# A hybrid encoder layer on one core: the value products of a pair of attention heads, issued block by block or as one chain

## The chip, the core and the metric

The kernel runs on one core of a Trainium2 chip. The metric is the device time of one execution in microseconds (us), lower is better. TensorE (PE) multiplies matrices, VectorE (DVE), ScalarE (ACT) and GpSimd (POOL) do the work on rows, and SyncE (SP) issues every DMA of this kernel from one queue, in the order of the program. Each engine runs its instructions in the order in which they stand.

## The reference, cut to what matters

One layer reads 16 meta tokens, a prompt of 512 tokens and a sample of 2048 tokens, all float32 with 1024 features. One input projection feeds two groups of heads, and one output projection adds their result to the input.

```
proj = rms_norm(h) @ w_in                      # 1024 x 4624
q_m, k_m, v_m, o_m, z_m, gates, q_a, k_a, v_a, z_a = split(proj)
# group A: mLSTM in both directions, 4 heads of 128
q_m, k_m = silu(conv5(q_m, k_m));  h_m = scan_forward + scan_backward
y_m = rms_norm(sigmoid(o_m) * h_m) * silu(z_m)
# group B: attention on a grid of 64 columns, 8 heads of 64, window 8 rows x 16 columns + meta keys
s = rms_norm(q_a) . rms_norm(k_a) / 8 + bias   # masked to the window
y_a = (softmax(s) @ v_a) * silu(z_a)
out = h + concat(y_m, y_a) @ w_out
```

## The kernel before, in words

The program is written as generators that are stepped in turn (`weave`); a scheduler then puts the recorded instructions of each engine into an order of its own, which is fixed before the kernel runs. What stands in the tables of order below is that fixed order.

*Projections* (`mmt`, `mmf`, L233) multiply blocks of tokens by groups of 256 columns of `w_in`, three matmuls for each product (high and low parts). There are 7600 of them. The first half of the tokens comes first, then the second half; the last to come are the columns of the prompt. *Attention* (L478 on) runs over five windows of 8 grid rows (the name of a window's kind stands in `WINS`), and in each over four pairs of heads: 20 pairs. Windows 1 and 2 run beside the projections of the first half, windows 3, 4 and 0 beside those of the second half; the small window 0 is the last. For each pair the kernel

- loads keys `kt`, values `vt`, queries `qt` and bias rows `R`, transposes the keys into `kps` (two halves, L502) and splits them on ACT and DVE into `Ks`, and does the same for the queries (`qps`, L512);
- for each of four blocks of query columns, b = 1, 2, 0, 3, and each of the two heads: scores `sps` on PE (L546), bias and minimum on DVE (L549), exponential on ACT (L550), reciprocal and scaling on DVE (L551, L552), three or four transposes into `pps` (L555), and a copy into a buffer `pt` on ACT (head 0, L558) or DVE (head 1, L560);
- after the two heads of a block, multiplies with the values: `py<-pt,vt` (L564), 3 or 4 chunks by 2 heads. The stationary operand has 64 columns, and each head writes its own 64 partitions of `py`, so one head takes one half of the array's columns and the other head the other half. All other matmuls of this kernel load 128 columns (the meta tokens' 48 and a few small ones apart);
- at the end multiplies `py` with the gate rows `zt` (L571) and stores them.

There are three `pt` buffers, one `vt`, and two banks of PSUM for the tag `c`, which `kps` and `py` take in turn.

*The mLSTM* has a backward part, `mlstm_back`: 15 steps over the chunks of the sample from the last to the first, then 3 for the prompt. A step loads `kT` and `v` (one buffer each, tags of the pool `bp`), transposes the keys (`kpm`, L671), scales them on ACT (`kw`, L674), multiplies (`ups`, L684), updates the state `CB` on DVE (L690) and stores it (`cbs`, L704). It begins when all the sample's keys and values are through, and each step needs the one before. The forward part (`hps`, L781 and L783) and the output projections (`ops`, L843) come last: chunk 0 of the sample needs the state that the last backward step of the sample stored (`CBl<-cbs`). The attention's pool of SBUF is given back when attention is through (`tstack.close()`); the output weights (`wor`, eight loads of 512 KB through one buffer) and the buffers of the forward part are laid into it.

Of the kernel before, what the change touches and what calls it, by code (L numbers as in the profile page):

```python
# [26 lines left out]
# window geometry of the attention: kinds of row groups (P, first, middle, last)  # L27
# kind: (key rows, first key row, first query row, grid rows, row offset in the bias table)
# [39 lines left out]
def bcast(ap, n):  # L68
    """A DRAM row read by n partitions."""
    return bass.AP(tensor=ap.tensor, offset=ap.offset, ap=[[0, n]] + [list(x) for x in ap.ap])  # L70


def view(ap, dims):
    """A tile's partitions with free dimensions of one's own."""
    return bass.AP(tensor=ap.tensor, offset=ap.offset, ap=[list(ap.ap[0])] + [list(x) for x in dims])


class Rot:
    """a pool whose tags turn over n tiles (or k times as many)"""
# [8 lines left out]
class Run:  # L88
# [4 lines left out]
    def setup(self):  # L93
        nc, a = self.nc, self.a
        self.const = cp = self.ctx.enter_context(self.tc.tile_pool(name="const", bufs=1))
        self.dram = dp = self.ctx.enter_context(self.tc.tile_pool(name="scr", bufs=1, space=bass.MemoryType.DRAM))
        PS = bass.MemoryType.PSUM
        ent = self.ctx.enter_context
        self.ps_mm = ent(self.tc.tile_pool(name="ps_mm", bufs=2, space=PS))
        self.ps_a = ent(self.tc.tile_pool(name="ps_a", bufs=2, space=PS))  # L100
        self.ps_b = ent(self.tc.tile_pool(name="ps_b", bufs=2, space=PS))
        self.ps_c = ent(self.tc.tile_pool(name="ps_c", bufs=2, space=PS))

        self.ident = cp.tile([128, 128], F32, name="ident")
        make_identity(nc, self.ident)
        self.bg_rep = cp.tile([128, 16], F32, name="bg_rep")
        self.cw = cp.tile([128, 8, 5], F32, name="cw")
        self.gq = cp.tile([128, 1], F32, name="gq")
        self.gk = cp.tile([128, 1], F32, name="gk")
        self.mg = cp.tile([128, 4], F32, name="mg")  # L110
        self.gcol = cp.tile([84, 2, 8], F32, name="gcol")
        self.one = cp.tile([1, 128], F32, name="one")
        nc.vector.memset(self.one, 1.0)
        # gates: type, chunk (P 0-3, S 4-19, meta 20), head
        self.gates = cp.tile([128, 4, 21, 4], F32, name="gates")
        for ty, val in ((0, NEG), (1, 1e4), (2, NEG), (3, 1e4)):
            nc.gpsimd.memset(self.gates[:, ty, 20, :], val)
        self.kv = set()
        self.tails = cp.tile([128, 8, 4], F32, name="tails")
        self.mraw = cp.tile([128, 8, 20], F32, name="mraw")  # L120
        nc.vector.memset(self.mraw, 0.0)

        d = lambda name, shape, dt=F32: dp.tile(shape, dt, name=name)
        self.x2 = d("x2", [10, 128, KT * 128])
        # token rows: P 0-511, S 512-2559, meta 2560-2575
        # attention: by blocks of grid columns (16 or 8), then grid rows (P 0-7, S 8-39)
        self.qs = d("qs", [4, 40 * 16, 512])
        self.ks = d("ks", [8, 40 * 8, 512])
        self.vs = d("vs", [8, 40 * 8, 512])
        self.kmeta = d("kmeta", [8, 8, 512])  # L130
        self.vmeta = d("vmeta", [8, 8, 512])
        self.zs = d("zs", [512, 2560])
        self.vms = d("vms", [2576, 512])
        self.ozs = d("ozs", [2560, 1024])
        self.kqs = {"P": d("kqsP", [1024, NM + LP]), "S": d("kqsS", [1024, NM + LS])}
        self.yas = d("yas", [512, 2560])
        self.rp = d("rp", [88, 94])
        self.Rd = d("Rd", [128, 169, 32])
        self.Mrow = d("Mrow", [2, 84 * 128])
        self.cbs = d("cbs", [20, 128, 4 * 129])  # L140
# [12 lines left out]
    def bias_table(self, pool):  # L153
        """for a query at (qr, qc) of its tile: a head's relative key rows (15 of 22) and columns"""
        nc, s = self.nc, self.rp
        t = pool.tile([128, D], F32, tag="x", name="rpt", bufs=3)
        nc.sync.dma_start(out=t[:88, :94], in_=self.a["rpbp"].rearrange("h (i a) j -> (h i) (a j)", a=2))
        nc.sync.dma_start(out=s, in_=t[:88, :94])
        for qr in range(8):
            src = bass.AP(tensor=s.tensor, offset=s.offset + (7 - qr) * 47 + 15, ap=[[47, 169], [-1, 16], [1, 32]])  # L160
            nc.sync.dma_start(out=self.Rd[qr * 16:(qr + 1) * 16, :, :].rearrange("q i j -> i q j"), in_=src)
            yield

# [16 lines left out]
    def xprep(self, pool, srcs, put):  # L180
        """srcs: DRAM rows of up to 128 tokens each; put(i, k0, psum) takes the transposes."""
# [25 lines left out]
    def split(self, hi, lo, ps):  # L207
        """hi: ps rounded to float32r; lo: what is left."""
        self.nc.scalar.copy(out=hi, in_=ps)
        self.nc.vector.tensor_tensor(out=lo, in0=ps, in1=hi.bitcast(F32), op=ALU.subtract)  # L210

# [15 lines left out]
    def mm3(self, ps, st, mv, n_k=KT):  # L227
        """ps = sum over k of st^T mv, both as (hi, lo)."""
# [7 lines left out]
    # token-major product: 128 tokens by n columns  # L236
# [6 lines left out]
    # token-major product of the meta tokens: hi on the first 16 partitions, lo on those from 32  # L243
# [13 lines left out]
    # feature-major product: 128 columns by a block's tokens  # L257
# [82 lines left out]
    def phase_a1(self, blocks, pool, first=None):  # L340
        """first: weights of the first two column groups, which are then taken block by block"""
# [13 lines left out]
    def phase_a1_z(self, blocks, pool, done):  # L355
        """done: gets the groups of columns that are through"""
# [18 lines left out]
    def conv(self, pool, raw, n, ct):  # L375
        """silu of the five taps: n outputs from n + 4 inputs."""
# [10 lines left out]
    def phase_a2(self, blocks, pool, free=None):  # L387
        """free: is told of each block that is no longer needed"""
# [86 lines left out]
    def attention(self, pool, wins, zdone):  # L475
        nc, a = self.nc, self.a
        for wi in wins:
# [6 lines left out]
            for pair in range(4):  # L484
                f0 = pair * 128
                kt = pool.tile([128, 8, 128], F32, tag="kt", name="kt", bufs=1)
                vt = pool.tile([128, 8, 128], F32, tag="vt", name="vt", bufs=1)
# [9 lines left out]
                # keys: head A as [hi; lo], head B as [lo; hi]  # L497
# [11 lines left out]
                # queries: hi and lo, each twice over the partitions  # L509
# [13 lines left out]
                py = self.ps_c.tile([128, 512], F32, tag="c", name="py")  # L523
                biases = {}
                for b in (1, 2, 0, 3):
# [5 lines left out]
                    pts = []  # L531
                    for hh in range(2):
# [23 lines left out]
                        pt = pool.tile([128, 512], F32, tag="pt", name="pt", bufs=3)  # L556
# [4 lines left out]
                        pts.append(pt)  # L561
                    for c in range(nch):
                        for hh in range(2):
                            nc.tensor.matmul(py[hh * 64:(hh + 1) * 64, b * 128:(b + 1) * 128], vt[:nk, cbs[c], hh * 64:(hh + 1) * 64], pts[hh][:nk, c * 128:(c + 1) * 128], start=c == 0, stop=c == nch - 1)  # L564
                    yield
# [10 lines left out]
    def gate_rows(self, pool):  # L576
# [9 lines left out]
        for d in range(2):  # L586
            big = pool.tile([128, 8, 128], F32, tag="vt", name=f"gbig{d}", bufs=1)
# [23 lines left out]
            # rows: b_L, A_L, m before, m after  # L611
# [54 lines left out]
    def wk(self, pool, kT, n, d, c):  # L666
        """token-major keys times the chunk's state weights."""
# [9 lines left out]
    def state(self, pool, kw, v, n, d, c, old, new):  # L677
        """new = decay * old + kw^T [v 1]"""
# [13 lines left out]
    def mlstm_back(self, pool, seq):  # L692
        """states that the backward direction has on entering each chunk."""
# [13 lines left out]
    def mlstm_first(self, pool, keep, seq):  # L707
        """the state that the meta tokens leave"""
# [7 lines left out]
    def mlstm(self, pools, rest, first, C, pre0, pre1, out_proj):  # L716
        """pools, rest: of the chunks in turn; first: gives a sequence's first state; C, pre0, pre1: for the first chunks"""
# [10 lines left out]
    def mlstm_pre(self, pool, seq, i):  # L728
        """what a chunk needs beside the states"""
# [119 lines left out]
def weave(main, *others, until=None):  # L849
    """Steps main to its end, or until that of one of the others: (generator, steps per step of main)."""  # L850
# [19 lines left out]
def hymba(ctx, tc, a):  # L870
# [12 lines left out]
    def block_t(where, tag, n, **kw):  # L883
        """by tiles of 128 tokens"""
# [74 lines left out]
    def reload():  # L959
        """the second part's x into the blocks of the first as they come free"""  # L960
# [110 lines left out]
```

## Time and profile before

| what | value |
|---|---|
| device time, three runs | 1788.88, 1791.68, 1792.33 us; median 1791.68 |
| span of the profiled execution, first to last instruction | 1788.1 us |
| PE busy | 1727.4 us, 97% of the span |
| DVE, ACT, POOL busy | 62%, 44%, 28% of the span |
| granted TensorE clock, mean | 0.992 of full speed |

The profile gives one execution, and its span is the time that it shows; it lies 3.6 us under the median of the runs, within their spread of 3.5 us at the lower end. "Busy" of PE is the union of the modelled durations of its matmuls, which overlap, so what a matmul costs is read from the distance between the starts of neighbouring matmuls and not from its duration. A line such as `py<-pt,vt x10` stands for ten records; a float32 product (`py`, `ups`, `hps`, `sm`) leaves two records for each matmul, a transpose or a product of the split parts leaves one.

### The profile page before, as it was taken

What the parts mean: (1) busy time and instruction counts of PE and PEld (TensorE: products, weight loads), DVE (VectorE), ACT (ScalarE), POOL (GpSimd) and SP (SyncE); (2) the same over time, 40 slices, a digit from 0 to 9 for tenths busy, and PEclk for the clock granted to TensorE, in tenths of its full rate; (3) what the DMA queues carried; (4) which work ended last, traced back from release to release, by engine and by line L of the source; (5) the groups of instructions that cost most, each with busy time, mean ns of one, the idle gap of its engine ahead of it and who ended that gap; (6) DMA issues with size and microseconds to landing.
All of it is one profiled execution on the core that took longest, in us unless ns stands there. A gap on an engine that the chain in (4) does not pass through costs nothing. (4 is left out here: it accounts for less than half of the span.)

```text
span 1788.1 us, 33369 instructions
## 1 busy us (share of the span) xinstructions
PE 1727.4 (97%) x12316; PEld 1554.0 (87%) x12316; DVE 1115.2 (62%) x2984; ACT 779.4 (44%) x1835; POOL 496.9 (28%) x503
## 2 busy tenths in 40 slices
PE   6999999999999999999999999999989899989999
PEld 6999998889889998999888888889878888878887
DVE  8896124654654369861249889876564578776772
ACT  5442232433444265422236666665554444443430
POOL 4012222223312253212124443432443222221210
PEclk9999999999999999999999999999999999999999
DMA  5367422324234363423334454444777765546531
GB/s 185 122 225 169 124 82 91 98 61 122 85 98 127 95 196 115 122 71 88 94 114 128 124 168 127 121 133 123 238 242 210 239 197 180 190 165 200 176 121 71
DMA packets 265986, 251.93 MB, mean 141 GB/s; under 512 B 38663, under 2 KB 228943, under 8 KB 265823
## 3 DMA queue, kind: packets, MB, share of 16 engines
q1 hardware_dynamic: 265822, 249.80, 46.2%
q8 instruction: 97, 1.59, 0.4%
q14 instruction: 67, 0.54, 0.1%
HBM read 176.34 MB, written 76.17 MB: 141 GB/s over the span
## 5 line engine op out<-in xcount | busy, mean ns | idle before, releaser
L233 PE MATMUL mmt<-wh,xah 128*128 128x256 f32 (+1 forms) x1536 | 437.9, 285 | 5.8 <-ACT sq L319 2.8
L233 PE MATMUL mmt<-wl,xah 128*128 128x256 f32 (+1 forms) x1536 | 438.0, 285 | 0.0
L233 PE MATMUL mmt<-wh,xal 128*128 128x256 f32 (+1 forms) x1536 | 436.5, 284 | 0.0
L224 POOL TENSOR_TENSOR wl<-wr,wh 128x512 fp32r<-128x512 f32 (+1 forms) x184 | 252.1, 1383 | 626.3 <-ACT wh L223 597.0
L233 PEld LDWEIGHTS mmt<-wh,xah 128*128 128x128 f32 x1536 | 289.9, 189 | 9.5 <-ACT sq L319 3.9
L233 PEld LDWEIGHTS mmt<-wh,xal 128*128 128x128 f32 x1536 | 291.0, 189 | 1.9 <-issue 1.0
L233 PEld LDWEIGHTS mmt<-wl,xah 128*128 128x128 f32 x1536 | 289.8, 189 | 2.3 <-issue 1.5
L537 POOL TENSOR_TENSOR bias<-R,amask 128x384 f32<-128x384 f32 (+5 forms) x120 | 111.8, 944 | 246.7 <-DVE mx L549 129.5
L223 ACT CAST wh<-wr 128x512 fp32r<-128x512 f32 (+1 forms) x184 | 109.8, 621 | 141.8 <-DMA wr<-in_w_in 121.1
L382 DVE SCALAR_TENSOR_TENSOR acc<-craw,cw,acc 128x256 f32<-128x256 f32 (+2 forms) x192 | 156.3, 814 | 24.1 <-ACT acc L380 19.7
L233 PE MATMUL mmf<-xah,wh 128*128 128x512 f32 x384 | 153.5, 400 | 1.4 <-DVE zt L368 1.2
L233 PE MATMUL mmf<-xal,wh 128*128 128x512 f32 x384 | 153.4, 399 | 0.0
L233 PE MATMUL mmf<-xah,wl 128*128 128x512 f32 x384 | 152.7, 398 | 0.0
L550 ACT ACTIVATE s<-s,mx 128x384 f32<-128x384 f32 (+5 forms) x160 | 96.1, 601 | 82.7 <-DVE mx L549 73.1
L233 PE MATMUL mmt<-wh,xbh 128*128 128x256 f32 (+1 forms) x384 | 113.0, 294 | 5.9 <-ACT sq L325 3.6
L233 PE MATMUL mmt<-wh,xbl 128*128 128x256 f32 (+1 forms) x384 | 112.9, 294 | 0.0
L564 PE MATMUL py<-pt,vt 128*64 128x128 f32 (+3 forms) x1120 | 110.3, 283 | 2.0 <-DVE pt L560 2.0
L233 PE MATMUL mmt<-wl,xbh 128*128 128x256 f32 (+1 forms) x384 | 111.8, 291 | 0.0
L549 DVE CUSTOM_DVE_ANT_0 s<-sps,bias 128x384 f32<-128x384 f32 (+5 forms) x160 | 84.5, 538 | 37.8 <-PE sps L546 34.4
L564 PEld LDWEIGHTS py<-pt,vt 128*64 128x64 f32 (+3 forms) x1120 | 72.9, 136 | 30.4 <-issue 12.7
L520 DVE SCALAR_TENSOR_TENSOR ql<-qps,gq,qh 64x512 fp32r<-64x512 f32 x80 | 59.9, 749 | 62.9 <-ACT qh L519 61.4
L552 DVE TENSOR_SCALAR s<-s,mx 128x384 f32<-128x384 f32 (+5 forms) x160 | 96.7, 606 | 3.1
(238 smaller groups left out, 3795.3 us busy)
## 6 DMA issues: line engine op xcount, KB each, us to landing
wr<-in_w_in SPq DMA_DIRECT2D x176, 256.0 KB
ozs<-vbuf SPq DMA_DIRECT2D x40, 256.0 KB
X<-Mrow SPq DMA_DIRECT2D x20, 512.0 KB
oz<-ozs SPq DMA_DIRECT2D x20, 512.0 KB
v<-vms SPq DMA_DIRECT2D x38, 256.0 KB
x<-in_xs SPq DMA_DIRECT2D x16, 512.0 KB
kq<-kqsS SPq DMA_DIRECT2D x16, 512.0 KB
xres<-in_xs SPq DMA_DIRECT2D x16, 512.0 KB
```

What stands on the lines that cost most here:

```text
L223: nc.scalar.copy(out=wh[:, ks, :n], in_=wr[:, :, :n])
L224: nc.gpsimd.tensor_tensor(out=wl[:, ks, :n], in0=wr[:, :, :n], in1=wh.bitcast(F32)[:, ks, :n], op=ALU.subtract)
L233: nc.tensor.matmul(ps, st(s, k), mv(m, k), start=i == 0, stop=i == last)
L382: nc.vector.scalar_tensor_tensor(out=acc[:, :n], in0=raw[:, d:d + n], scalar=self.cw[:, ct, d:d + 1], in1=acc[:, :n], op0=ALU.mult, op1=AL ...
L520: nc.vector.scalar_tensor_tensor(out=ql[to], in0=qps[hp], scalar=self.gq[hp], in1=qh[hp].bitcast(F32), op0=ALU.mult, op1=ALU.subtract)
L537: nc.gpsimd.tensor_tensor(out=view(bias[:, :], dims), in0=view(rb, [[8, nch], [32, nr + 1], [1, 8]]), in1=view(mask[:, bt, :], dims), op=A ...
L549: nc.vector.tensor_tensor_reduce(out=s[:, :n], in0=ps[:, o:o + n], in1=bias[:, :n], op0=ALU.add, op1=ALU.min, scale=-1.0, scalar=BIG, accu ...
L550: nc.scalar.activation(out=s[:, :n], in_=s[:, :n], func=AF.Exp, scale=-1.0, bias=mx[:, 0:1], accum_out=mx[:, 1:2])
L552: nc.vector.tensor_scalar(out=s[:, :n], in0=s[:, :n], scalar1=mx[:, 2:3], scalar2=0.5, op0=ALU.mult, op1=ALU.mult)
L564: nc.tensor.matmul(py[hh * 64:(hh + 1) * 64, b * 128:(b + 1) * 128], vt[:nk, cbs[c], hh * 64:(hh + 1) * 64], pts[hh][:nk, c * 128:(c + 1) ...
```

## The change

Nothing that is computed changes. The value products of a pair are held back until the probabilities of all four blocks lie in `pt` buffers, and are then issued as 28 matmuls in a row, blocks in the order 3, 0, 2, 1, heads 1 and 0 in turn, with an order between neighbours that is given to the scheduler (`behind`: order alone, no semaphore). `py` is taken from PSUM only then. The `pt` buffers become five of 384 and five of 512 columns, `vt` gets a second buffer, and the room for them comes from the DMA scratch, which is set to 1024 bytes. There is one step (`yield`) more for each pair.

```diff
+    def behind(self, m, prev):
+        if prev is not None:
+            self.tc.add_manual_dep(m.ins, prev.ins.name, mybir.DependencyInfo(mybir.DependencyClass.NoSync, mybir.DependencyReason.DATA), reason="in turn")
+        return m
...
-                vt = pool.tile([128, 8, 128], F32, tag="vt", name="vt", bufs=1)
+                vt = pool.tile([128, 8, 128], F32, tag="vt", name="vt", bufs=2)
...
-                py = self.ps_c.tile([128, 512], F32, tag="c", name="py")
                 biases = {}
+                pts = {}
                 for b in (1, 2, 0, 3):
...
-                    pts = []
+                    pts[b] = []
...
-                        pt = pool.tile([128, 512], F32, tag="pt", name="pt", bufs=3)
+                        pt = pool.tile([128, nch * 128], F32, tag=f"pt{nch}", name="pt", bufs=5)
...
-                        pts.append(pt)
+                        pts[b].append(pt)
+                    yield
+                py = self.ps_c.tile([128, 512], F32, tag="c", name="py")
+                prev = None
+                for b in (3, 0, 2, 1):
+                    nch = len(CHUNKS[b])
                     for c in range(nch):
-                        for hh in range(2):
-                            nc.tensor.matmul(py[hh * 64:(hh + 1) * 64, b * 128:(b + 1) * 128], vt[:nk, cbs[c], hh * 64:(hh + 1) * 64], pts[hh][:nk, c * 128:(c + 1) * 128], start=c == 0, stop=c == nch - 1)
-                    yield
+                        for hh in (1, 0):
+                            m = nc.tensor.matmul(py[hh * 64:(hh + 1) * 64, b * 128:(b + 1) * 128], vt[:nk, CHUNKS[b][c], hh * 64:(hh + 1) * 64], pts[b][hh][:nk, c * 128:(c + 1) * 128], start=c == 0, stop=c == nch - 1)
+                            prev = self.behind(m, prev)
+                yield
...
-            big = pool.tile([128, 8, 128], F32, tag="vt", name=f"gbig{d}", bufs=1)
+            big = pool.tile([128, 8, 128], F32, tag="vt", name=f"gbig{d}", bufs=2)
...
-    nc = bacc.Bacc("TRN2", target_bir_lowering=False, num_devices=1)
+    nc = bacc.Bacc("TRN2", target_bir_lowering=False, num_devices=1, dynamic_dma_scratch_size=1024)
```

The scheduler orders all engines anew. Three places of PE's order show what moves. The first is the middle of a pair in the second half of the projections; before, it reads so:

```order
L233 MATMUL mmt<-wl,xbh 128x256
L564 MATMUL py<-pt,vt 64x128 x5
L555 MATMUL pps<-ident,s 104x128 x3
L564 MATMUL py<-pt,vt 64x128
L546 MATMUL sps<-Ks,ql 128x288
L233 MATMUL mmt<-wh,xbl 128x256
```

and after the change, in the same stage, a whole pair stands in one place:

```order
L239 MATMUL mmt<-wl,xah 128x256
L239 MATMUL mmt<-wh,xal 128x256
L575 MATMUL py<-pt,vt 64x128 x28
L508 MATMUL kps<-ident,kt 128x128 x4
L239 MATMUL mmt<-wh,xah 128x256
```

The 560 value products stand in 155 groups before (74 of one, one of two, 37 of five, 5 of six, 35 of seven, 3 of eight) and in 23 after (17 of 28, and 9 with 19, 1 with 27, 10 with 18).

The second place is the end of the last pair but one and the whole last pair. Before, the last group of all stands among projections, and 754 of the 7600 follow it:

```order
L671 MATMUL kpm<-ident,kT 128x128 x4
L233 MATMUL mmf<-xah,wl 128x512
L233 MATMUL mmf<-xah,wh 128x512
L233 MATMUL mmf<-xal,wh 128x512
L564 MATMUL py<-pt,vt 64x128 x5
L233 MATMUL mmf<-xah,wl 128x512
```

After the change the last projection (`mmt`, second row) comes before the last two chains, and the last pair's keys (`kps`) come behind the chain of the pair before:

```order
L552 MATMUL sps<-Ks,ql 128x256
L239 MATMUL mmt<-wh,xal 128x256
L561 MATMUL pps<-ident,s 72x128 x3
L518 MATMUL qps<-ident,qt 128x128 x4
L561 MATMUL pps<-ident,s 72x128 x9
L683 MATMUL kpm<-ident,kT 128x128 x4
L696 MATMUL ups<-v_14124,kw 128x129 x2
L575 MATMUL py<-pt,vt 64x128 x10
L696 MATMUL ups<-v_14124,kw 128x129 x2
L575 MATMUL py<-pt,vt 64x128 x18
L508 MATMUL kps<-ident,kt 128x72 x8
L552 MATMUL sps<-Ks,qh 128x288
```

So the projections that followed attention before now lie inside it. The third place is the backward part. Before, projections stand between its steps (this is the last step of the sample; `v_15636` is its buffer):

```order
L233 MATMUL mmt<-wh,xah 128x256
L684 MATMUL ups<-v_15636,kw 128x129 x2
L233 MATMUL mmt<-wl,xah 128x256
L233 MATMUL mmt<-wh,xal 128x256
L233 MATMUL mmt<-wh,xah 128x256
L684 MATMUL ups<-v_15636,kw 128x129 x2
```

After, the last chain is followed by the fifth of the sample's 15 steps (`v_14613`) and its successors with nearly nothing between them, down to `v_15636`:

```order
L575 MATMUL py<-pt,vt 64x128 x28
L696 MATMUL ups<-v_14613,kw 128x129 x4
L683 MATMUL kpm<-ident,kT 128x128 x4
L696 MATMUL ups<-v_14723,kw 128x129 x4
L683 MATMUL kpm<-ident,kT 128x128 x4
L753 MATMUL sm<-kq 128x128 x8
L696 MATMUL ups<-v_14828,kw 128x129 x4
L683 MATMUL kpm<-ident,kT 128x128 x4
L696 MATMUL ups<-v_14907,kw 128x129 x4
```

So eleven of the 15 backward steps of the sample, the meta tokens' product and the three steps of the prompt stand behind the last chain; two stand ahead of the last projection. On SP the loads of the output weights (`wor`) stand behind the last pair's store in both orders, and in the new one among the loads of these backward steps.

## Rows read from the trace of the kernel before

**Rows 1.** The page: span, busy time of PE and DVE, clock in 40 slices.
```profile
span 1788.1 us, 33369 instructions
...
PE 1727.4 (97%) x12316; PEld 1554.0 (87%) x12316; DVE 1115.2 (62%) x2984; ACT 779.4 (44%) x1835; POOL 496.9 (28%) x503
...
PEclk9999999999999999999999999999999999999999
```

**Rows 2.** Stages: stretch, length, busy time of each engine, clock, DMA share, GB/s.
```profile
203.70:757.40 553.70, 548.15 (x4021) 498.30 (x4019) 301.46 (x683) 228.22 (x475) 159.91 (x166) 1.00 0.36 107
925.60:1261.30 335.70, 335.45 (x2638) 291.23 (x2636) 266.86 (x630) 204.72 (x453) 126.75 (x152) 1.00 0.45 131
1261.30:1407.70 146.40, 136.84 (x958) 125.75 (x956) 76.19 (x120) 71.45 (x159) 60.02 (x65) 0.99 0.75 227
1407.70:1434.30 26.60, 19.41 (x135) 17.44 (x134) 21.27 (x62) 14.67 (x47) 7.80 (x9) 0.92 0.89 283
1434.30:1788.10 353.80, 340.38 (x1922) 288.50 (x1921) 239.68 (x760) 140.52 (x474) 76.36 (x49) 0.99 0.51 164
```

**Rows 3.** Timeline of PE: start, length, what; one value product among projections.
```profile
279.11 0.40 PE L233 MATMUL mmf<-xal,wh 128*128 128x512 f32 x1
279.34 0.39 PE L233 MATMUL mmf<-xah,wl 128*128 128x512 f32 x1
279.67 0.43 PE L564 MATMUL py<-pt,vt 96*64 96x128 f32 x2
280.03 0.39 PE L233 MATMUL mmf<-xbh,wh 128*128 128x256 f32 x1
280.25 0.28 PE L233 MATMUL mmf<-xbl,wh 128*128 128x256 f32 x1
280.37 0.28 PE L233 MATMUL mmf<-xbh,wl 128*128 128x256 f32 x1
```

**Rows 4.** Timeline of PE: five value products among projections.
```profile
282.86 0.28 PE L233 MATMUL mmf<-xbh,wl 128*128 128x256 f32 x1
283.07 0.87 PE L564 MATMUL py<-pt,vt 96*64 96x128 f32 x10
283.87 0.50 PE L233 MATMUL mmf<-xah,wh 128*128 128x512 f32 x1
284.21 0.40 PE L233 MATMUL mmf<-xal,wh 128*128 128x512 f32 x1
```

**Rows 5.** First and last value product and output product, by tile.
```profile
L564 PE MATMUL py<-pt,vt x1120: 272/273/324, 279.7 to 1261.3; 128*64 128x128 f32 x74, 96*64 96x128 f32 x38, 104*64 104x128 f32 x38, 72*64 72x128 f32 x37
...
L843 PE MATMUL ops<-woh,yh x160: 391/397/775, 1434.3 to 1780.2; 128*128 128x512 f32 x160
```

**Rows 6.** The chain of work: a backward step, then chunk 0 (start, length).
```profile
1374.33 4.45 DMA v<-vms
1378.78 0.14 issue
1378.91 0.68 PE ups L684 x4
1379.60 0.36 PE mmt L233 x3
1379.96 0.45 PE ups L684 x4
1380.40 2.24 PE mmt L233 x19
1382.64 0.44 PE kpm L671 x4
...
1410.10 5.73 DMA v<-vms
...
1418.72 2.53 issue
1421.25 1.21 DVE X L747
```

**Rows 7.** DVE in 1214 to 1262 us, the last pair: busy, mean ns of one.
```profile
L549 DVE CUSTOM_DVE_ANT_0 s<-sps,bias 128x216 f32<-128x216 f32 x7 | 2.6, 382 | 2.4 <-PE sps L546 1.7 <-POOL bias L537 0.5
L552 DVE TENSOR_SCALAR s<-s,mx 128x216 f32<-128x216 f32 x7 | 2.3, 333 | 0.2
L560 DVE COPY pt<-pps 72x384 f32<-72x384 f32 x4 | 2.2, 554 | 7.0 <-PE pps L555 7.0
L508 DVE SCALAR_TENSOR_TENSOR Ks<-kps,gk,Ks 64x288 fp32r<-64x288 f32 x4 | 2.1, 516 | 0.3 <-ACT Ks L507 0.2
L560 DVE COPY pt<-pps 72x512 f32<-72x512 f32 x3 | 2.1, 687 | 1.2 <-PE pps L555 1.2
L551 DVE RECIPROCAL mx<-mx 128x1 f32<-128x1 f32 x11 | 1.8, 160 | 1.7 <-ACT s L550 1.7
L549 DVE CUSTOM_DVE_ANT_0 s<-sps,bias 128x288 f32<-128x288 f32 x4 | 1.7, 453 | 0.8 <-PE sps L546 0.8
L552 DVE TENSOR_SCALAR s<-s,mx 128x288 f32<-128x288 f32 x4 | 1.6, 392 | 0.1
```

**Rows 8.** PE in 1214 to 1262 us: transposes of the last pair.
```profile
L555 PE MATMUL pps<-ident,s 128*72 128x128 f32 x44 | 7.2, 278 | 0.0
```

**Rows 9.** First start of a forward product, and of the sample's last backward step.
```profile
L781 PE MATMUL hps<-v,X x320: 271/275/422, 1407.8 to 1744.7; 128*128 128x129 f32 x160
...
L684 PE MATMUL ups<-v,kw x64: 268/275/423, 1385.8 to 1434.2; 128*128 128x129 f32 x56, 16*128 16x129 f32 x8
```

## The prediction, made before the changed kernel ran

> **What bounds the kernel now.** I read the page first: PE is busy 97% of 1788.1 us, DVE 62%, at a clock that is full in all 40 slices but a few short drops [rows 1]. Then the same by stages: in the two stretches that hold attention, PE has work for 548.15 of 553.70 us and 335.45 of 335.70 us, so there PE is the bound and every microsecond that it needs less is a microsecond of time; DVE has 266.86 of the 335.70 us and is not far behind [rows 2]. After attention (1261.3 us) PE still has 136.84 of 146.40 us, in which the last 754 projections run; from 1407.7 to 1434.3 us, up to the first output product, it has 19.41 of 26.60 us; the rest, 353.8 us, is the mLSTM's forward part [rows 2, 5]. Value products run from 279.7 to 1261.3 us [rows 5]; 110 us of durations stand behind them, but these overlap and say little, so I priced them from the starts of their neighbours.
>
> **What a group of value products costs.** One product among projections: from the start of the projection ahead (279.34) to that of the second one behind (280.25) pass 0.91 us; the two projections alone would take 0.23 + 0.12 (starts of their like: 279.11 to 279.34, 280.25 to 280.37). So the group of one costs 0.56 us [rows 3]. Five products: 282.86 to 284.21 is 1.35 us, less 0.12 and 0.23: 1.00 us [rows 4]. The two heads write different halves of the array's columns, and their records start together, so I count products in pairs (slots): one slot in the group of one, three in the group of five. Two equations: a slot costs (1.00 - 0.56) / 2 = 0.22 us, and a group 0.34 us on top, whatever its size: entering and leaving the half-width form costs as much as three products in pairs.
>
> Before there are 155 groups; their slots are 74 + 1 + 37 x 3 + 5 x 3 + 35 x 4 + 3 x 4 = 353. After there are 23 groups and 17 x 14 + 5 + 10 + 1 + 14 + 5 + 9 = 282 slots. Saved: 132 x 0.34 + 71 x 0.22 = 45 + 15.5 = 60 us of PE. The lower bound is 45 us if the new chains pair no better than the old groups, the upper 62 us.
>
> **What else the edits cost.** The `behind` order adds no instruction and no wait. The smaller DMA scratch: all DMAs here are issued by SP in order, nothing in the rows draws on the scratch; I take nothing, and no bound can be read. The second `vt` lets loads come earlier, where PE waits for none now [rows 2]. The held-back `pt`: 8 tiles are in use at the chain and there are ten, so a next pair can begin its softmax with two more and then waits for the chain; PE has projections to fill that, while there are some. That is the point on which the sum turns: attention now takes more projections per pair, and by the new order none is left for the last pair.
>
> **The end of attention, worked out.** Before, the last projection ends at 1407.7, where the first forward product starts [rows 2, 9]. In the new order PE reaches that point with less behind it:
> - 60 us saved;
> - still to come: three chains (3 x 0.34 + 28 x 0.22 = 7 us) and 40 transposes with the scores and keys of the last pair. 44 transposes are 7.2 us of overlapping durations [rows 8]; I take 8 us for all, 15 us with the chains;
> - still to come: 15 of the 17 steps that the backward part (meta tokens counted in) had made by 1407.7; a step is 0.45 + 0.45 + 0.44 = 1.34 us of PE [rows 6], so 20 us.
>
> 1407.7 - 60 - 15 - 20 = 1313; of the 9.6 us in which PE waited in that stage [rows 2] I take 2 off: 1311. From here the work is no longer hidden:
> - the rest of the last pair but one: 3.8 us of chain, a backward step, some transposes, 2 us for the last `pt` copy: 1319;
> - the last pair alone. DVE: keys 2.1, bias and minimum 4 x 0.38 + 1.7, scaling 4 x 0.33 + 1.6, reciprocals 8 x 0.16, half of the copies 2 x 0.55 + 2 x 0.69 [rows 7], in all about 12; 4 us to fill and drain the pipeline through PE and ACT; chain 0.34 + 14 x 0.22 = 3.4. So 1339. Before, the same pair ran beside projections that were wanted anyway;
> - the backward steps. Each has one `v` buffer, so a step is load, products, release: 4.45 + 0.14 + 0.90 + 0.1 = 5.6 us [rows 6]. The fifth step's `v` is there; ten more of the sample end at 1339 + 1 + 56 = 1396. Before, they were spread over 1261 to 1386 us beside projections and cost nothing;
> - meta tokens and three steps of the prompt, 4 x 5.6 less the last products: the last `v` lands at 1417.5. Before, from the landing of that `v` (1410.10 + 5.73) to the first output product (1434.3) passed 18.5 us, of which 2.53 + 1.21 were a wait for DVE's `X` [rows 5, 6] whose load can now be early: I take 14.8. First output product: 1432.3.
>
> The eight `wor` loads and their splitting go beside these steps (one load to a step or two) and end before. From the first output product on, PE's order is that of before: 353.8 us. Sum: 1786 us of span, 2 us less than before. The median of the runs lies 3.6 us over this span; I add the same: **1789 us**. Of 60 us saved, 58 are given back, because what hid the last pair and the backward part has been used up earlier.
>
> **Rivals.**
> - *The end closes up* (0.23). The projections' loads are gone from the queue and a `v` load may take 3.3 us (my estimate; 4.45 was measured at 227 GB/s [rows 2, 6]): a step of 4.4 us, 14 steps 17 us less, and 4 to 8 us less where PE waited for weights. Span 1763, time 1766. For it: most of the traffic goes. Against: `wor`, `X` and `kq`, 512 KB each, come into the same stretch.
> - *Loads collide* (0.09), the case on the other side. SP issues `v` behind `wor`, `X`, `oz`; at 283 GB/s a `v` took 5.73 us [rows 2, 6]. Then a step is 6.9 us, and 14 of them 18 us more: 1807. It is slower than before by 0.2% from a step of 6.0 us on.
> - [...]
> - *The saving is not there* (0.04): if the 0.34 us belonged to each product's neighbours and not to entering and leaving, only the 15 us of better pairing remain, and the end is exposed all the same: 1835.
>
> **How the numbers follow.** My forecast has 0.56, and a range of its own of 1778 to 1801: 5 us in where the last pair ends, 0.4 us in a step. 0.2% is 3.6 us, about what a measurement of this kernel can tell from no change (the runs lie 3.5 us apart). Round 1789 that makes 0.19 faster, 0.21 within, 0.16 slower. With the rivals: faster 0.19 + 0.23 = 0.42; same 0.21; slower 0.16 + 0.09 + 0.08 + 0.04 = 0.37. For 8 in 10 I go from 1763, which takes in most of the first rival, to 1810, which takes in collisions and the slow clock and leaves out the last.
>
> **What would show it.** Right: PE's last projection starts near 1311 us; chains of 28 take 3.4 us; between the last chain and the first output product PE is busy for less than half, and waits for `v<-vms` about every 5.6 us; first output product near 1432. Wrong in the saving: a chain of 28 longer than 4 us, or the last projection after 1330. Wrong in the end: the stretch from the last chain to the first output product clearly under 80 or over 105 us (93 by my sum). Wrong outright: new waits of PE inside the attention stages (for `pt`, `vt` or the bias rows), where I count none.

## The result, and the profile after

The changed kernel takes **1821.2 us** (median of four runs, 1816.2 to 1822.7), the kernel before beside it 1792.0: 1.5% slower (ratio 1.0154, interval 1.0125 to 1.0184). The forecast was 1789 with a range up to 1810. The page of the profiled execution, against [rows 1]:

```profile
span 1820.9 us, 33314 instructions
...
PE 1708.7 (94%) x12316; PEld 1566.7 (86%) x12316; DVE 1126.9 (62%) x2984; ACT 777.4 (43%) x1835; POOL 494.3 (27%) x503
...
PEclk9999999999999999999999999999975699999999
```

PE is busy for 19 us less in a span that is 33 us longer, and three of the 40 slices have lost clock. Where they lie is read from first and last starts by tile (count: shortest/median/longest ns, first to last start), as in [rows 5]:

```profile
L239 PE MATMUL mmt<-wh,xal x1536: 274/281/428, 33.7 to 1325.4; 128*128 128x256 f32 x176, 128*128 128x272 f32 x16
L575 PE MATMUL py<-pt,vt x1120: 272/273/476, 322.8 to 1361.6; 128*64 128x128 f32 x74, 96*64 96x128 f32 x38, 104*64 104x128 f32 x38, 72*64 72x128 f32 x37
L855 PE MATMUL ops<-woh,yh x160: 390/397/506, 1463.6 to 1813.0; 128*128 128x512 f32 x160
```

The projections end 82 us earlier than before (1325.4 against 1407.7), yet the output products begin 29 us later (1463.6 against 1434.3). The value products, which ended 146 us ahead of the last projection, now end 36 us behind it. The stages from there (columns as in [rows 2]): the last pairs, the backward part, the middle of it, the rest:

```profile
1325.40:1361.60 36.20, 27.62 (x208) 22.48 (x209) 20.51 (x63) 19.08 (x50) 8.98 (x12) 0.72 0.64 201
1361.80:1463.60 101.80, 64.18 (x311) 54.28 (x309) 51.39 (x133) 42.85 (x129) 7.47 (x20) 0.61 0.67 203
1388.00:1426.00 38.00, 22.60 (x88) 18.10 (x88) 14.56 (x34) 10.77 (x31) 0.74 (x7) 0.50 0.58 172
1463.60:1820.90 357.30, 340.25 (x1923) 287.81 (x1921) 238.97 (x757) 138.70 (x467) 77.36 (x49) 0.99 0.49 159
```

So the end was bare, as forecast: no projections were left to fill the pauses of PE. In its middle the granted clock was 0.50 of full speed. Why were there no projections left? The timeline of PE at the end of a pair in the second half:

```profile
951.01 3.28 PE L575 MATMUL py<-pt,vt 128*64 128x128 f32 x56 [0.24 <-DVE pt L566]
954.22 0.66 PE L508 MATMUL kps<-ident,kt 128*128 128x128 f32 x4
957.43 0.60 PE L508 MATMUL kps<-ident,kt 128*128 128x128 f32 x4
```

The next pair's keys `kps` begin when the chain is through, and so it is for nearly every pair of the second half (the next keys start at 994.2 and 1035.3). So the pairs run one after the other, 40 us from one to the next, against 27 to 30 us before (last value products at 966.4, 993.4, 1023.6). There the next pair's keys were through ahead of the pair's last value products (timeline of PE, before):

```profile
956.32 0.60 PE L502 MATMUL kps<-ident,kt 128*128 128x128 f32 x4
965.76 0.87 PE L564 MATMUL py<-pt,vt 128*64 128x128 f32 x10
```

I took the ten `pt` buffers for what holds a pair back. My theory now: `kps` and `py` take the two PSUM banks of one tag in turn. Before, `py` took its bank at the first block, and the next pair's `kps` went through the other bank during the pair. Now `py` takes it at the chain, and `kps`, which come behind it in the program, have to wait for that. Rivals: the held-back buffers, or the chains themselves.

### The profile page after: what moved, and what is told of

It is laid out like the page before. It is cut to its first block, busy times and chain, and to the rows that moved or that the text cites. A ratio compares the mean times of both kernels' runs of the same rounds, so it can differ in the third digit from the quotient of the medians.

```text
span 1820.9 us, 33314 instructions
## 1 busy us (share of the span) xinstructions
PE 1708.7 (94%) x12316; PEld 1566.7 (86%) x12316; DVE 1126.9 (62%) x2984; ACT 777.4 (43%) x1835; POOL 494.3 (27%) x503
## 3 DMA queue, kind: packets, MB, share of 16 engines
q1 hardware_dynamic: 265822, 249.80, 45.4%
## 5 line engine op out<-in xcount | busy, mean ns | idle before, releaser
L558 DVE TENSOR_SCALAR s<-s,mx 128x384 f32<-128x384 f32 (+5 forms) x160 | 103.1, 646 | 3.1
L758 POOL TENSOR_TENSOR qw<-qw,kq 128x1024 f32<-128x1024 f32 (+1 forms) x20 | 63.1, 3155 | 123.0 <-ACT qw L757 114.5
L561 PE MATMUL pps<-ident,s 128*128 128x128 f32 (+3 forms) x560 | 86.6, 275 | 10.5 <-DVE s L558 8.0
```

The source lines that it names most:

```text
L558: nc.vector.tensor_scalar(out=s[:, :n], in0=s[:, :n], scalar1=mx[:, 2:3], scalar2=0.5, op0=ALU.mult, op1=ALU.mult)
L561: nc.tensor.transpose(pp[:nk, c * 128:(c + 1) * 128], s[:, c * nk:(c + 1) * nk], self.ident)
L758: nc.gpsimd.tensor_tensor(out=qw[:, :nd], in0=qw[:, :nd], in1=qT.unsqueeze(1).to_broadcast([128, nd, 4, 128]), op=ALU.mult)
```

## The experiments

The difference of each is to the kernel before as run beside it (1794.5 us for e1 to e4, 1793.0 for e5 to e8, 1792.9 for e9 to e11).

| run | us | ratio, interval |
|---|---|---|
| e1 `py` from another tag | 1763.8 | 0.9832, 0.9800 to 0.9863 |
| e2 groups of one block | 1790.1 | 0.9964, 0.9944 to 0.9983 |
| e3 buffers alone | 1793.8 | 0.9997, 0.9984 to 1.0010 |
| e4 pairs in turn, small groups | 1853.7 | 1.0325, 1.0297 to 1.0353 |
| e5 = e1, heads apart | 1777.5 | 0.9915, 0.9884 to 0.9947 |
| e6 = changed, two load buffers | 1809.4 | 1.0089, 1.0054 to 1.0124 |
| e7 = changed, 12 products added | 1847.1 | 1.0291, 1.0268 to 1.0314 |
| e8 = e1, two load buffers | 1765.1 | 0.9841, 0.9817 to 0.9864 |
| e9 = changed, 5 products added | 1821.1 | 1.0154, 1.0131 to 1.0176 |
| e10 = e1, backward steps earlier | 1773.0 | 0.9877, 0.9859 to 0.9894 |
| e11 = e1, eight `pt` | 1766.3 | 0.9846, 0.9827 to 0.9865 |

**e1: `py` from the tag of `pps`.**

```diff
-                py = self.ps_c.tile([128, 512], F32, tag="c", name="py")
+                py = self.ps_b.tile([128, 512], F32, tag="t", name="py")
```

> The changed kernel, with one edit: the value products' PSUM tile py comes from the two banks of the transposes pps and no longer from the two banks that it shares with the next pair's keys kps. Chains of 28 stay. Theory (turn of banks: kps of a pair stands behind the chain of the pair before because both take banks of one tag in turn, so pairs run one after the other, attention uses up the projections and the end is exposed): pairs overlap again, in the new order 450 projections follow the last chain and 13 backward steps come before the last projection, so the end is covered and the 52 to 58 us of saved value products remain: 1735 to 1750 us. Rival (ten probability buffers, eight of them held until the chain, keep the pairs apart on the chip, whatever the order says): PE then waits inside attention for the copies, 1800 us or more. Second rival (the chain itself costs more than the separate groups): no better than 1790 us.

1763.8 us, 31 less than before and 57 less than the change. With nothing but the tag changed, the keys of the next pair stand ahead of the chain again, 10 us here (timeline of PE, e1):

```profile
967.48 0.60 PE L508 MATMUL kps<-ident,kt 128*128 128x128 f32 x4
977.88 3.28 PE L575 MATMUL py<-pt,vt 128*64 128x128 f32 x56
```

The turn of banks is the cause of the serial pairs. The time is still 14 us above what I expected. The tile rows and the window of the bare end of e1 say where:

```profile
L239 PE MATMUL mmt<-wh,xal x1536: 274/281/428, 33.7 to 1354.8; 128*128 128x256 f32 x176, 128*128 128x272 f32 x16
L855 PE MATMUL ops<-woh,yh x160: 390/397/535, 1404.9 to 1752.3; 128*128 128x512 f32 x160
1354.80:1404.90 50.10, 30.42 (x187) 27.17 (x186) 22.30 (x81) 22.56 (x74) 9.14 (x13) 0.76 0.81 240
```

The last projection comes 52.9 us earlier than before, which is the 52 to 58 of the saving. From it to the first output product pass 50.1 us instead of 26.6 [rows 2]: six backward steps (the prompt's and the meta tokens' counted in) follow it instead of two. That is where most of the missing gain lies.

**e2: groups of one block, nothing held back.** In the block's loop:

```diff
+                    prev = None
                     for c in range(nch):
-                        for hh in range(2):
-                            nc.tensor.matmul(py[...], ...)
+                        for hh in (1, 0):
+                            m = nc.tensor.matmul(py[...], ...)
+                            prev = self.behind(m, prev)
```

> The kernel before, with one edit: the value products of one block of queries (6 or 8) are given an order among themselves, so that they stand together; nothing is held back over blocks, three probability buffers as before. 84 groups in place of 155, some 281 slots in place of 353. Theory (0.34 us for each group, 0.22 us for each slot, end covered: 13 of 18 backward steps stand ahead of the last projection): 71 x 0.34 + 72 x 0.22 = 40 us less than before, of which up to 5 us are lost at the end: 1750 to 1758 us. Rival (the price lies in the number of products alone and not in entering and leaving): 16 us less, 1776 us.

Only 4 us less than before: the expectation failed. The groups did save; the last projection comes 25 us earlier than before. The missing 15 us of my 40 are in part a wait: a group that stands together has to wait for the later `pt` (waits of PE until the last projection; 2.0 us in the whole kernel before), and what is behind it on PE waits too: all pauses of PE ahead of the last projection sum to 53.6 us, against 39.8 before.

```profile
PE py L571 <- DVE pt L566: 8.8, 6, 3.7
...
L239 PE MATMUL mmt<-wh,xal x1536: 274/281/420, 33.6 to 1383.0; 128*128 128x256 f32 x176, 128*128 128x272 f32 x16
L851 PE MATMUL ops<-woh,yh x160: 390/397/498, 1434.3 to 1782.9; 128*128 128x512 f32 x160
```

And the end took the rest: 51.3 us from the last projection to the first output product, 24.7 more than before, with six steps left as in e1. I had allowed 5 us for that. (The profiled run took 1792.7 us; the ten runs of e2 lie between 1780.5 and 1793.8.)

**e3: the second `vt` and the smaller scratch alone**, on the kernel before.

```diff
-                vt = pool.tile([128, 8, 128], F32, tag="vt", name="vt", bufs=1)
+                vt = pool.tile([128, 8, 128], F32, tag="vt", name="vt", bufs=2)
...
-    nc = bacc.Bacc("TRN2", target_bir_lowering=False, num_devices=1)
+    nc = bacc.Bacc("TRN2", target_bir_lowering=False, num_devices=1, dynamic_dma_scratch_size=1024)
```

> The kernel before with the second vt buffer and the smaller DMA scratch of the change, nothing else. Theory: both cost nothing and bring nothing: within 0.2% of before. Rival (the smaller scratch slows the issue of DMAs, or the earlier loads of values collide with others): 3 us or more slower, which would then be part of the loss of the change.

No difference (interval 0.16% down to 0.10% up): both are free, as forecast.

**e4: small groups as before, pairs in turn.** `last` is the pair's last value product:

```diff
-                        nc.tensor.transpose(ps[:, c * nk:(c + 1) * nk], ...)
+                        self.behind(nc.tensor.transpose(ps[:, c * nk:(c + 1) * nk], ...), last)
```

> The kernel before with small groups of value products as they were (156 groups), and one order added: the keys kps of a pair stand behind the last value product of the pair before. In the new order the last projections come within the last pair and one backward step ahead of the last projection, much as after the change, while the value products keep their price. Theory (the loss is the exposed end): the end is as bare as after the change and nothing is saved: the time of the change plus the 52 to 58 us that its chains save, less up to 20 us since half of the last pair is still covered: 1850 to 1878 us. Rival (what the change lost lies in the chains or in the held-back buffers): no slower than 1800 us.

1853.7 us: as the theory had it. With before, e1 and the change it fills a table of two by two:

| us | pairs overlap | pairs in turn | difference |
|---|---|---|---|
| small groups | 1794.5 (before) | 1853.7 (e4) | +59.2 |
| chains of 28 | 1763.8 (e1) | 1821.2 (the change) | +57.4 |
| difference | -30.7 | -32.5 | |

The two effects add: the chains bring 31 to 33 us net whichever way the pairs run, and running the pairs in turn costs 57 to 59 whichever way the products stand. (The change ran beside a kernel before of 1792.0 us; put on 1794.5 by its ratio it would stand at 1822.1.)

**e11: eight `pt` buffers instead of ten**, in e1.

```diff
-                        pt = pool.tile([128, nch * 128], F32, tag=f"pt{nch}", name="pt", bufs=5)
+                        pt = pool.tile([128, nch * 128], F32, tag=f"pt{nch}", name="pt", bufs=4)
```

> The kernel of e1 with four probability buffers of each size instead of five: exactly the eight that a chain reads, so that the next pair's first copy waits for the chain. Its order on PE is that of e1. Theory (the buffers didn't keep the pairs apart; the turn of the banks did): within 0.4% of e1, 1757 to 1770 us. Rival (the held-back buffers set the distance of pairs): the next pair's copies stall its transposes, 20 pairs by 1 us and more, 1785 us or above.

1766.3 us, within 0.2% of e1, and the next pair's keys still stand 10 us ahead of the chain (972.5 against 982.9): the held-back buffers are not what kept the pairs apart.

**e5: heads apart**, in e1.

```diff
-                    for c in range(nch):
-                        for hh in (1, 0):
+                    for hh in (1, 0):
+                        for c in range(nch):
```

> The kernel of e1, with the 28 products of a chain issued block by block, all of one head and then all of the other, instead of the two heads in turn. Theory (two heads in turn write different halves of the columns and run side by side, so the price is per slot of two, 0.22 us): 14 slots become 28 in each of 20 pairs, 20 x 14 x 0.22 = 62 us more than e1: about 1825 us. Rival (the records only start together, the products run one after the other anyway): no change, 1764 us.

14 us slower than e1, not 62: neither theory nor rival. A chain in e1 and in e5 (timeline of PE; start, length):

```profile
1008.62 0.28 PE L239 MATMUL mmt<-wh,xal 128*128 128x256 f32 x1
1008.83 3.28 PE L575 MATMUL py<-pt,vt 128*64 128x128 f32 x56
1012.04 0.50 PE L552 MATMUL sps<-Ks,qh 128*128 128x512 f32 x1
```
```profile
1012.97 3.88 PE L575 MATMUL py<-pt,vt 128*64 128x128 f32 x56
1016.78 0.50 PE L552 MATMUL sps<-Ks,qh 128*128 128x512 f32 x1
```

3.81 us instead of 3.21; 20 times 0.60 are 12 of the 14 us. Counting the records of `py` in the middle of a chain (2 us) and at its end (0.6 us), first e5, then e1:

```profile
1013.50:1015.50 2.00, 2.00 (x39) 2.00 (x36) 0.00 (x0) 1.00 0.00 0
1016.20:1016.80 0.60, 0.60 (x8) 0.40 (x4) 0.00 (x0) 1.00 0.00 0
```
```profile
1009.50:1011.50 2.00, 2.00 (x41) 2.00 (x38) 0.00 (x0) 1.00 0.03 8
1011.30:1011.90 0.60, 0.60 (x16) 0.56 (x12) 0.00 (x0) 1.00 0.00 0
```

In the middle both run at one pace (39 and 41 records). At the end of e5, where only one head's products are left, the pace is half (8 against 16). So by these counts the two heads do run side by side, 0.22 us for two; but they need not stand in turn for it: the products of one head overlap with the block of the other behind them, and what stands alone is mainly the rest at the end.

**e6: two buffers for the backward part's loads**, in the change.

```diff
-        kT = pool.tile([128, 4, 128], "kT")
+        kT = pool.tile([128, 4, 128], "kT", 2)
...
-        v = pool.tile([128, 4, 129], "v1")
+        v = pool.tile([128, 4, 129], "v1", b)
```

(`b` is 2 in the backward part; and `vt` with one buffer, for room)

> The changed kernel with two buffers each for the backward part's kT and v loads; the room comes from the second vt buffer, which is taken back to one. Pairs stay in turn, the end stays bare. Theory (a bare step is release, load of v 3.1 us, products 2.1 us, one after the other, because there is one v buffer): the load goes beside the products of the step before, a step falls from 5.4 to 3.2 to 3.6 us, 11 to 14 steps give back 20 to 30 us: 1791 to 1801 us. Rival (PE at half clock, DVE or the queue of loads bounds the step): within 5 us of 1821.

1809.4 us, 12 less than the change (15 by the spans of the profiled runs, 1805.9 against 1820.9); 20 to 30 were expected. The chain of work in the changed kernel, and then in e6:

```profile
1399.23 2.08 PE ups L696 x8
...
1401.36 3.08 DMA v<-vms
1404.44 0.14 issue
1404.58 2.08 PE ups L696 x8
```
```profile
1405.96 2.06 PE ups L696 x8
1408.03 0.97 PE kpm L683 x4
1409.08 0.38 ACT kw L686
1409.45 0.09 issue
1409.55 2.08 PE ups L696 x8
```

The load is out of the chain, and a step falls from 5.35 to 3.6 us, as the theory said. From the last value product (1366.6) to the first output product (1447.7) it is 81 us instead of 102. Of these 21 us, 5 were lost ahead of it (the last value product comes 5.0 us later than in the change, the last projection 6.2); why, I have not tested. What is left of the step is mostly PE's own work at a granted clock of 0.56 (1391 to 1424 us): 2.06 us for eight records, which took 1.13 us before (0.68 and 0.45 [rows 6]) and which I had priced at 0.90.

**e7 and e9: PE kept busy in the bare end**, in the change. In `state`, behind the update (12 in e7, 5 in e9; `two` holds the step's two PSUM tiles, and the added products write columns of them that nobody reads):

```diff
+        for j in range(more):
+            nc.tensor.matmul(two[j % 2][:, j // 2 % 2, 130:256], self.ident, new[:, j % 4, 0:126], start=True, stop=True)
```

> The changed kernel, with 12 products added behind the products of each of the last 11 backward steps of the sample and the three of the prompt; they read the new state and write columns of PSUM that nobody reads, and stand where PE waits for the next v. Theory (the bare steps run at half clock since PE pauses in each; kept busy it keeps its clock and the 8 product records of a step take 0.9 us and not 2.1): 14 x 1.2 = 17 us less than the change, 1804 us, and the granted clock of the stretch from the last chain to the first output product near full. Rival (the clock of the end costs nothing, since the load of v sets the step): 1821 us or up to 15 us more, by the added work.

> As e7, with 5 added products behind each of the 14 steps instead of 12, so that they end before the next load of v does. Theory (the half clock costs 1.2 us a step): where the granted clock of the bare stretch rises above that of the change, the step falls below 5.4 us, by 1.2 us if the clock is full: up to 17 us less than the change, 1804 us. Rival (a few products in the pause don't lift the clock, or the load of kT and the scaling behind it set the step as soon as the products are short): 1815 to 1830 us.

e7 is 26 us slower than the change and e9 equal to it. The clock did rise (windows of e7, then of e9, inside the bare end):

```profile
1390.00:1441.00 51.00, 41.31 (x282) 35.84 (x281) 18.04 (x40) 14.01 (x34) 0.84 (x8) 0.93 0.60 184
```
```profile
1390.00:1426.00 36.00, 25.23 (x147) 21.79 (x146) 14.33 (x32) 10.93 (x28) 0.73 (x7) 0.84 0.70 215
```

The granted clock of the stretch is 0.93 and 0.84 instead of 0.50, with PE busy for 41.31 of 51.00 and 25.23 of 36.00 us instead of 22.60 of 38.00. (Busy time alone does not set it: e6 had 0.56 with PE busy for 27.54 of 33.00 us.) But the added work stands between a step's products and the next step's keys (timeline of PE, e7, then e9):

```profile
1397.22 4.33 PE L706 MATMUL ups<-CB,ident 128*128 128x126 f32 x24
1401.39 0.60 PE L683 MATMUL kpm<-ident,kT 128*128 128x128 f32 x4
1402.56 1.44 PE L698 MATMUL ups<-v,kw 128*128 128x129 f32 x8 [0.56 <-ACT kw L686]
```
```profile
1401.47 1.42 PE L706 MATMUL ups<-CB,ident 128*128 128x126 f32 x10 [0.26 <-DVE CB L704]
1402.72 0.60 PE L683 MATMUL kpm<-ident,kT 128*128 128x128 f32 x4
1405.61 1.13 PE L698 MATMUL ups<-v,kw 128*128 128x129 f32 x8 [2.29 <-DMA v<-vms]
```

In e7 the next step's keys come only behind twelve products. In e9 the eight records of a step's products take 1.13 us from 1400.08 on (2.06 in the change), and the stretch from the last value product (1358.1) to the first output product (1455.6) is 97.5 us instead of 102.0, but behind it 3 us more pass than after the change; the medians are equal. These stretches can't be compared cleanly, because the scheduler has also put the first output product earlier in PE's order: from it on stand 1959 of PE's records in e9 and 2002 in e7, against 1923 after the change. So these runs show that the clock of these steps rises with added work, and not what the low clock costs: neither gained, but the filling work and the other order of the end can't be told apart in them.

**e8 and e10: can e1 be improved?** e8 is e1 with the edit of e6; e10 is e1 with

```diff
-    weave(R.phase_a2(h2[:2], ap), (att, 2), (ahead, 0.4))
+    weave(R.phase_a2(h2[:2], ap), (att, 2), (ahead, 0.7))
```

> The kernel of e1 (value products' bank from another tag) and two buffers for the backward part's kT and v as in e6, vt back to one. Theory: five of the 18 backward steps stood behind the last projection in e1; their loads now run ahead, 5 x 2 us less and some of the 14 us in which e1 waited for v: 1750 to 1756 us. Rival (these loads wait for their place in the queue of SP, not for a buffer): 1764 us.

> The kernel of e1 with the backward part stepped at 0.7 instead of 0.4 beside the projections of the second half, its rate elsewhere as before. In the order 8 instead of 4 steps stand ahead of the last chain and 14.5 instead of 13 ahead of the last projection. Theory (what e1 still loses is the 50 us from the last projection to the first output product, 26.6 before): each step less behind the last projection is worth 4 us: 1755 to 1760 us. Rival (more loads beside attention cost as much, or the wait for the prompt's keys sets the end): 1764 us.

Neither is faster than e1: 1765.1 us is the same, 1773.0 is slower by 0.5%, barely clear of the noise (the two intervals overlap slightly). In e10 the first output product comes 8 us earlier than in e1, but it also stands earlier in PE's order: 1978 of PE's records are left from there on, against 1923 in e1, and this rest takes 18 us longer (355.3 us in e1; the window of e10):

```profile
1397.20:1771.00 373.80, 349.91 (x1978) 297.65 (x1977) 244.81 (x782) 144.43 (x488) 76.54 (x52) 0.98 0.48 156
```

So e10 moved work behind that product and did not shorten the end. e1 remains the fastest here, 1.7% faster than before.

## Why the prediction was wrong

*The saving* was right within its bounds of 45 to 62 us: 60 us forecast, 52.9 us at the last projection of e1, where the pairs overlap. (Four backward steps fewer stand ahead of it than before, 5.4 us at the price of the forecast, and the pauses of PE ahead of it sum to 5.6 us more, 45.4 against 39.8; the two about cancel.) The prices held too: by 0.34 + 14 x 0.22 a chain costs 3.42 us; from the projection ahead of e1's chain to the second `sps` behind it (1012.38) pass 3.76 us, less 0.12 and 0.23 for the neighbours: 3.41. The 0.34 us for a group could also belong to the float32 form and not to the half width. The trace of before speaks against that: two float32 products of 128 columns (`ups`) among projections take 0.45 us by the same reckoning (1385.63 to 1386.32 is 0.69, less twice 0.12), 0.11 for each of the four records and nothing on top. (The start of this document has it wrong that nearly all other matmuls load 128 columns: 336 of the 560 transposes `pps` load 72, 96 or 104, still more than the 64 of `py`.)

*The mechanism* was right in its outline: the end is bare, and eats more than the saving. Its size was not. The step that failed is the one on what the edits cost, "a next pair can begin its softmax with two more and then waits for the chain; PE has projections to fill that", for which I counted no new wait of PE. In its place the runs show two things. The next pair can't even transpose its keys, since these wait for `py`'s turn, and pairs run one after the other (e1, e4, e11); I had read from the order that pairs took more projections, and put it down to the wrong resource. And PE does wait inside attention, 21 us instead of 4, which is the largest part of the miss. The other parts lie in the bare end, where every stretch came out longer than its term. Term by term, against the span of 1786 (the span misses by 35 us and the time by 32, since the median lies 0.3 us over the span here and not 3.6 as I had added):

- **The last projection**: 1311 forecast, 1325.4 measured, +14. I counted no new waits inside attention and had called them what would be "wrong outright". They are there (waits of PE from 200 us to the last projection, after):

```profile
PE kps L508 <- DVE zt L583: 5.6, 3, 2.8
PE pps L561 <- DVE s L558: 5.5, 6, 2.5
PE sps L552 <- DVE mx L555: 4.7, 3, 4.0
PE py L575 <- DVE pt L566: 2.8, 5, 1.0
```

  18.6 us in these four rows, 21 us with the smaller ones of attention; in the same stretch before, attention's instructions waited 3.7 us. Only the 5.6 us of `kps` hang on the banks' turn for certain: they are gone in e1. The others are not: with its pairs overlapping, e1 still has 17 us of waits of attention's instructions ahead of its last projection, so waits of this size come without pairs in turn as well, and what brings them was not tested. All pauses of PE ahead of the last projection sum to 48.6 us; the forecast had those of before, 39.8, less 2. That is 11 of the 14 us.
- **The last pair but one**: 1311 to 1319 forecast, 1325.4 to 1338.9 measured, +5.5; **the last pair**: 20 us forecast, 22.9 measured, +3 (the split of its keys holds PE for 3.8 us; timeline of PE, after):

```profile
1331.55 2.28 PE L575 MATMUL py<-pt,vt 72*64 72x128 f32 x20
1333.76 1.23 PE L696 MATMUL ups<-v,kw 128*128 128x129 f32 x4
1334.91 4.11 PE L575 MATMUL py<-pt,vt 72*64 72x128 f32 x36
1338.95 1.60 PE L508 MATMUL kps<-ident,kt 72*128 72x72 f32 x8
1344.37 0.61 PE L552 MATMUL sps<-Ks,qh 128*128 128x288 f32 x1 [3.81 <-DVE Ks L514]
```

  The chain ahead of these keys takes 6.2 us, not 3.4: the granted clock was 0.51 from 1331.55 to 1338.95.
- **The backward steps**: 93 us from the last chain to the first output product, 101.8 measured, +8.5, inside the 80 to 105 that I allowed. In the middle a step takes 5.4 us as forecast (5.6), by two errors that cancel, which is luck: the load takes 3.1 us instead of 4.45, as the rival "the end closes up" had it, and the products 2.08 instead of 0.90, at a granted clock of 0.50. The 8.5 us lie ahead of these steps and behind them. The third step behind the last chain starts 10.5 us after the second (1366.35 to 1376.85); in the chain of work ahead of its products stand, among shorter pieces, a load of `kT` of 5.25 us and 3.76 us of the forward part's `sm`. So the sample's last step ends 62 us behind the last chain and not 57. The meta tokens' and the prompt's steps and chunk 0 take the other 3.6 us; these I have not followed up. PE is busy for 64 of the 101.8 us, and not for less than half, at a mean clock of 0.61. The 0.08 among the chances and the slow clock that the range up to 1810 takes in were an estimate of mine that no run shows; what the runs showed is 0.50 granted for the 38 us from 1388 to 1426, where the products of a step cost 1.2 us more than I had priced and the shorter loads (1.4 us a step) took that back.
- **The forward part**: 353.8 forecast, 357.3 measured, +3.5; not followed up.

The sum is 14.4 + 5.5 + 3 + 8.5 + 3.5 = 35 us, the distance from 1786 to 1820.9. The rivals "loads collide" and "the saving is not there" are out: the loads of `v` in the chain became shorter for nearly all steps (3.0 to 4.7 us; one of the prompt's took 6.3), and e1 has the saving.

What stays open: what brings most of the new waits inside attention, what sets the granted clock in the bare end and how much 0.50 alone costs there (e7 and e9 could not separate it), and why e1's own end got no shorter by earlier loads or steps.

## What to carry to other kernels

Before work is held back, list every resource that it takes later than before, PSUM banks included: what stands behind it in the same turn is held back with it, here the next pair's keys, and that cost 57 us where the edit itself brought 31. Where an order is at hand, look not only at what moved but for what no longer overlaps, and ask which shared tag forces it. And work that is only free while something hides it has to be counted again whenever the hiding work is used up earlier.

## What the hardware showed that I had not expected

- Two heads' products of half width (64 columns each) overlapped even when they did not stand in turn: 3.81 us for a chain in e5 against 3.21 in e1, not the 6.2 us (28 x 0.22) that I estimate for one after the other. In the middle of a chain 39 records of `py` ran in 2 us (e5) against 41 (e1), at its end 8 against 16 in 0.6 us.
- In the bare end, steps of 5.4 us with eight product records, four transposes of keys and pauses of 0.3 to 2.2 us between them ran at a granted clock of 0.50 throughout (1388 to 1426 us); with ten more records in each step it was 0.84 (e9, 1390 to 1426 us), with twenty-four 0.93 (e7, 1390 to 1441 us), and neither made the kernel faster.
- By the prices above, a group of half-width products takes 0.34 us on top of its products, while two float32 products of full width among projections took nothing on top (0.45 us for two `ups`, before).
